# RG-LRU gates with both halves of a block in 128 rows, and a pair of tiles in stages

## The chip, the cores and the metric

The kernel runs on one core of a Trainium2 chip. The metric is the device time of one execution in microseconds (us), median over a few runs.

## The reference

One layer of a decoder trunk for 512 tokens of width 2048, all in fp32: an input projection, a group of RG-LRU recurrences (1024 features) beside a group of eight differential-attention heads, an output projection, a layer norm, a gated MLP with a short convolution, and a second layer norm. What the change touches is the recurrence:

```python
u = _causal_dwconv(rg_x, conv_w, conv_b)
ub = u.reshape(B, S, RG_BLOCKS, RG_BLOCK_DIM)          # 16 blocks of 64 features
r = jax.nn.sigmoid(jnp.einsum('bsgi,gij->bsgj', ub, wa).reshape(B, S, RG_WIDTH) + ba)
ig = jax.nn.sigmoid(jnp.einsum('bsgi,gij->bsgj', ub, wx).reshape(B, S, RG_WIDTH) + bx)
log_a = RG_C * r.astype(jnp.float32) * jax.nn.log_sigmoid(lam.astype(jnp.float32))
a = jnp.exp(log_a)
mult = jnp.sqrt(-jnp.expm1(2.0 * log_a))
bterm = mult * (ig * u).astype(jnp.float32)
_, h = lax.associative_scan(_lru_combine, (a, bterm), axis=1)
```

Each gate of a block is a product of the block's 64 features with a matrix of 64 x 64.

## The kernel before

Features lie in the 128 partitions and tokens in the 512 columns, so a tile of 128 features holds two blocks of 64. Every matmul operand is split into a high and a low half (`split`, lines 101 to 110: ScalarE copies the high half into the reduced format, VectorE subtracts it for the low half), and `mm3` (line 112) makes a product of three matmuls: high by high, low by high, high by low.

The weights come as raw tiles of 128 x 1024 over SyncE's queue, three buffers of them, and are split as they are wanted (`Weights`, lines 155 to 198). The split halves of a weight, `whi` and `wlo`, have three buffers each (W_BUFS): the fourth weight's split waits until TensorE is through with the first's. A weight of 128 x 1024 feeds eight products, 24 matmuls of 512 columns for a projection, 12 for each half of 512.

`PLAN` (line 69) is the order of the projections: values, queries and keys of a head (`qk`), recurrence inputs (`x`), output gates (`g`), and `rec`, the recurrence of a pair of tiles, four in all. Tasks that need several engines (a head's attention, a recurrence) are generators that `spawn` puts beside the projections with a delay; `tick` counts on a modelled time for each product and resumes a task when its time has come. So the text of the program is a mixture of products and small pieces of such tasks. From it a list scheduler in the framework makes the queue of each engine at build time, by the program's order and its own estimate of durations. An engine works its queue off in that order.

A recurrence before is one piece: `recurrence` (line 458) yields only at its end. It makes four gate products for the pair (two tiles by two gates, `mm3` at line 466, weights of 128 x 128 with zeros outside two blocks of 64 x 64), four sigmoids, and then for both tiles in step exp and tanh, the products on VectorE, the root, and two scans. The heads that run beside it have, at the end, a root and a reciprocal of the norm of the head's output (rs, lines 439 and 440), and at the head's start `qk_of` (line 500) makes q and k in halves of 64 rows: k_0 and k_1 hold a component's high half twice, one copied by `split`, the other at line 519, after VectorE's low half at line 518 has been taken.

Of the kernel before, what the change touches and what calls it, by code (L numbers as in the profile page):

```python
# [10 lines left out]
F32 = mybir.dt.float32  # L11
F32R = mybir.dt.float32r
AF = mybir.ActivationFunctionType
ALU = mybir.AluOpType
PSUM = bass.MemoryType.PSUM

P = 128
# [4 lines left out]
RGT = RG // P  # L22
H = 8
DH = 64
# [19 lines left out]
C_FB = C_FW + 2 * FT * 3  # L44
C_LQ = C_FB + 2 * FT
NC_ = C_LQ + 4 * DH


A_BUFS = 56
# [22 lines left out]
def f32(ap):  # L72
    return ap.bitcast(F32)
# [3 lines left out]
def trunk_kernel(ctx, tc, xT, w_qkg, w_v, gate_w, w_out0, w_out, w_up0, w_up, w_down, ln2, consts, out):  # L77
# [17 lines left out]
    def t_tile(dt=F32, name="t"):  # L95
        return tmp.tile([P, S], dt, tag="t", bufs=T_BUFS, name=name)
# [7 lines left out]
    def split(src, hi=None, lo=None, mk=a_tile):  # L104

        hi = mk(F32R, "hi") if hi is None else hi
        lo = mk(F32R, "lo") if lo is None else lo
        nc.scalar.activation(hi, src, AF.Copy)  # L108
        nc.vector.tensor_tensor(lo, src, f32(hi), ALU.subtract)  # L109
        return hi, lo  # L110

    def mm3(ps, w, x, first, last, onto=False):

        for n, (a, b) in enumerate(((w[0], x[0]), (w[0], x[1]), (w[1], x[0]))):
            nc.tensor.matmul(  # L115
                ps, a, b, start=first and n == 0, stop=last and n == 2, skip_group_check=onto
            )
# [85 lines left out]
    def col(i, n=1):  # L203
        return cst[:, i : i + n]
# [240 lines left out]
    def rg_in(j):  # L445
        ps = proj()
        uu = t_tile(F32, "uu")
        nc.scalar.activation(
            uu, ps, AF.Identity, scale=col(C_CONVW + 4 * j + 3), bias=col(C_CONVB + j)
        )  # L450
        for t in range(1, 4):
            nc.vector.scalar_tensor_tensor(
                uu[:, t:], ps[:, : S - t], col(C_CONVW + 4 * j + 3 - t), uu[:, t:],
                ALU.mult, ALU.add,
            )
        return uu, split(uu, mk=t_tile)

    def recurrence(j0, us, w):

        hi, lo = w  # L460
        gates = []
        for i, (uu, s) in enumerate(us):
            for g in range(2):
                c = slice((2 * i + g) * P, (2 * i + g + 1) * P)
                pg = bank()
                mm3(pg, (hi[:, c], lo[:, c]), s, True, True)
                gt = t_tile(F32, "gt")
                nc.scalar.activation(gt, pg, AF.Sigmoid, bias=col((C_BA, C_BX)[g] + j0 + i))  # L468
                gates.append(gt)
        ms, as_ = [], []  # L470
        for i in range(2):
            j, r = j0 + i, gates[2 * i]
            a = t_tile(F32, "a")
            nc.scalar.activation(a, r, AF.Exp, scale=c8[:, j : j + 1])  # L474

            nc.scalar.activation(r, r, AF.Tanh, scale=nc8[:, j : j + 1])
            as_.append(a)
        for i in range(2):
            uu, ig, r, a = us[i][0], gates[2 * i + 1], gates[2 * i], as_[i]
            nc.gpsimd.tensor_tensor(ig, ig, uu, ALU.mult)  # L480
            m = t_tile(F32, "m")
            nc.vector.tensor_tensor(m, a, a, ALU.mult)
            nc.vector.scalar_tensor_tensor(m, m, 1.0, r, ALU.add, ALU.mult)
            ms.append(m)
        for m in ms:
            nc.scalar.activation(m, m, AF.Sqrt)  # L486
        for i in range(2):
            nc.vector.tensor_tensor(ms[i], ms[i], gates[2 * i + 1], ALU.mult)
            hh = a_tile(F32, "hh")
            nc.vector.tensor_tensor_scan(hh, as_[i], ms[i], 0.0, ALU.mult, ALU.add)  # L490
            mix[j0 + i] = hh
        yield 0.0

    def rg_gate(j):
        ps = proj()
# [422 lines left out]
    j = 0  # L918
# [131 lines left out]
def _layout(inputs):  # L1050
    import numpy as np

    g = {k: np.asarray(v) for k, v in inputs.items()}
    f = np.float32

    def tiles(w, cols):

        k = w.shape[0] // P
        w = w.reshape(k, P, -1, P)
        return np.ascontiguousarray(w.transpose(2, 1, 0, 3)[cols]).reshape(len(cols), P, k * P)  # L1060

    a = {}
    a["xT"] = np.ascontiguousarray(g["x"][0].T).reshape(KT, P, S)
    w = g["w_in"][0]
    rgx, rgg = list(range(0, 8)), list(range(8, 16))
    qk = [t for h in range(H) for t in (16 + h, 24 + h)]
    a["w_qkg"] = tiles(w, qk + rgx + rgg)
    wv = w[:, 4096:].reshape(KT // 2, 2, P, 2, 512)
    a["w_v"] = np.ascontiguousarray(wv.transpose(3, 0, 2, 1, 4)).reshape(2, KT // 2, P, 1024)
    gw = np.zeros((RGT // 2, P, 2, 2, P), f)  # L1070
    for i, n in enumerate(("rg_gate_a_w", "rg_gate_x_w")):
        b = g[n][0].reshape(RGT // 2, 2, 2, 64, 64)
        gw[:, :64, :, i, :64] = b[:, :, 0].transpose(0, 2, 1, 3)
        gw[:, 64:, :, i, 64:] = b[:, :, 1].transpose(0, 2, 1, 3)
    a["gate_w"] = gw.reshape(RGT // 2, P, 4 * P)
    wo = g["w_out"][0].reshape(KT, P, D)[ORDER].reshape(D, D)
    a["w_out"] = tiles(wo, list(range(2, KT)))
    w = wo.reshape(KT // 4, 4, P, KT, P)[:, :, :, :2]
    a["w_out0"] = np.ascontiguousarray(w.transpose(0, 2, 1, 3, 4)).reshape(KT // 4, P, 1024)
    up = [t for i in range(FT) for t in (i, FT + i)]  # L1080
    a["w_up"] = tiles(g["w_up"][0], up[4:])
    w = g["w_up"][0].reshape(2, KT // 2, P, 2 * FT, P)[:, :, :, up[:4]]
    a["w_up0"] = np.ascontiguousarray(w.transpose(1, 2, 0, 3, 4)).reshape(KT // 2, P, 1024)
    wd = g["w_down"][0].reshape(FT // 2, 2, P, D // S, S)
    parts, at = [], 0
    for n in CHUNKS:
        w = wd[at // 2 : (at + n) // 2].transpose(3, 0, 2, 1, 4)
        parts.append(w.reshape(-1, P, 2 * S))
        at += n
    a["w_down"] = np.ascontiguousarray(np.concatenate(parts))  # L1090
    a["ln2"] = np.stack([g["ln_ffn_g"][0], g["ln_ffn_b"][0]]).astype(f)
    c = np.zeros((P, NC_), f)

    def put(at, v):
        c[:, at : at + v.shape[1]] = v

    put(C_CONVW, g["rg_conv_w"][0].reshape(4, RGT, P).transpose(2, 1, 0).reshape(P, -1))
    for at, n in ((C_CONVB, "rg_conv_b"), (C_BA, "rg_gate_a_b"), (C_BX, "rg_gate_x_b"),
                  (C_LAM, "rg_lambda"), (C_SUB, "subln_g"), (C_G1, "ln_mix_g"),
                  (C_B1, "ln_mix_b")):  # L1100
        put(at, g[n][0].reshape(-1, P).T)
    fw = g["ffn_conv_w"][0].reshape(3, 2 * FT, P)[:, up]
    put(C_FW, fw.transpose(2, 1, 0).reshape(P, -1))
    put(C_FB, g["ffn_conv_b"][0].reshape(2 * FT, P)[up].T)
    for i, n in enumerate(("lam_q1", "lam_k1", "lam_q2", "lam_k2")):
        put(C_LQ + i * DH, np.broadcast_to(g[n][0], (P, DH)))
    a["consts"] = c
    return a
# [23 lines left out]
```

## Time and profile before

| | us |
|---|---|
| median of 3 runs | 2069.66 (2069.61 to 2070.09) |
| the profiled execution | 2069.49 |
| its span | 2067.7 |
| TensorE busy | 2048.1 (99%) |
| VectorE busy | 1368.9 (66%) |
| ScalarE busy | 1039.5 (50%) |
| GpSimd busy | 181.4 (9%) |

The span is the time from the first to the last instruction; the rest of the execution lies around it. A busy share is a mean over all stages. Of TensorE's matmuls, the pitch from one start to the next is what counts, since they are pipelined: each lasts 0.39 us from start to end while the next one starts well before. The projections and attention, where the recurrences stand, take the first 530 us or so; the rest is the output projection and the MLP.

### The profile page before, as it was taken

What the parts mean: (1) busy time and instruction counts of PE and PEld (TensorE: products, weight loads), DVE (VectorE), ACT (ScalarE), POOL (GpSimd) and SP (SyncE); (2) the same over time, 40 slices, a digit from 0 to 9 for tenths busy, and PEclk for the clock granted to TensorE, in tenths of its full rate; (3) what the DMA queues carried; (4) which work ended last, traced back from release to release, by engine and by line L of the source; (5) the groups of instructions that cost most, each with busy time, mean ns of one, the idle gap of its engine ahead of it and who ended that gap; (6) DMA issues with size and microseconds to landing.
All of it is one profiled execution on the core that took longest, in us unless ns stands there. A gap on an engine that the chain in (4) does not pass through costs nothing.

```text
span 2067.7 us, 28020 instructions
## 1 busy us (share of the span) xinstructions
PE 2048.1 (99%) x10649; PEld 1757.5 (85%) x10649; DVE 1368.9 (66%) x2075; ACT 1039.5 (50%) x1651; POOL 181.4 (9%) x227
## 2 busy tenths in 40 slices
PE   9999999999999999999999999999999999999997
PEld 7888888888888899888888888888888888888886
DVE  6566645768334867888888888888888343333346
ACT  5475735668322656566565566566566232222232
POOL 1000000010122232001001000000100000000000
PEclk9999999999999999999999999999999999999999
DMA  6223222222443246576676676676678643242322
GB/s 221 97 72 97 73 93 85 87 82 91 144 128 128 76 125 167 153 189 171 167 192 170 166 188 176 165 187 178 164 184 283 225 139 116 92 142 92 112 82 82
DMA packets 98152, 288.46 MB, mean 140 GB/s; under 512 B 10209, under 2 KB 18401, under 8 KB 98017
## 3 DMA queue, kind: packets, MB, share of 16 engines
q1 hardware_dynamic: 86496, 244.71, 36.2%
q0 software_dynamic: 11520, 41.95, 11.9%
q8 instruction: 84, 1.38, 0.3%
q14 instruction: 52, 0.42, 0.1%
HBM read 266.70 MB, written 19.92 MB: 139 GB/s over the span
## 4 chain that ended last, share of the span: by engine, by line
PE 94%; ACT 3%; DVE 2%; DMA 1%; issue 1%; DVEq 0%; SPq 0%; ACTq 0%
PE ps L115 54%; PE ps L129 37%; PE ps L359 1%; ACT gt L468 0%; PE ps L360 0%; PE ps L765 0%; ACT s L371 0%; PE ps L389 0%; DVE lo L109 0%; DVE y L621 0%; DMA hid<-hidd 0%; ACT a L474 0%; ACT L486 0%; ACT L474 0%; ACT L468 0%
## 5 line engine op out<-in xcount | busy, mean ns | idle before, releaser
L109 DVE TENSOR_TENSOR wlo<-raw,whi 128x512 fp32r<-128x512 f32 (+1 forms) x676 | 605.2, 913 | 408.6 <-ACT whi L108 407.1
L108 ACT ACTIVATE whi<-raw 128x512 fp32r<-128x512 f32 (+1 forms) x676 | 525.3, 801 | 477.4 <-PE ps L115 376.6
L129 PE MATMUL ps<-hl,whi 128*128 128x512 f32 x1280 | 320.5, 392 | 0.0
L115 PE MATMUL ps<-wlo,hi 128*128 128x512 f32 x768 | 299.5, 390 | 0.6 <-DVE wlo L109 0.6
L115 PE MATMUL ps<-whi,hi 128*128 128x512 f32 x768 | 299.1, 390 | 0.3 <-ACT hi L108 0.3
L115 PE MATMUL ps<-hi,whi 128*128 128x512 f32 (+1 forms) x768 | 298.9, 389 | 0.0
L115 PE MATMUL ps<-whi,lo 128*128 128x512 f32 x768 | 298.7, 389 | 0.0
L115 PE MATMUL ps<-hi,wlo 128*128 128x512 f32 (+1 forms) x768 | 296.6, 386 | 1.2 <-DVE wlo L109 1.2
L115 PE MATMUL ps<-lo,whi 128*128 128x512 f32 (+1 forms) x768 | 296.2, 386 | 0.0
L129 PEld LDWEIGHTS ps<-hl,whi 128*128 128x128 f32 x1280 | 230.2, 189 | 41.1
L129 PE MATMUL ps<-x,whi 128*128 128x512 f32 x960 | 237.2, 389 | 0.0
L129 PEld LDWEIGHTS ps<-x,whi 128*128 128x128 f32 x960 | 180.1, 188 | 37.3
L129 PE MATMUL ps<-hl,wlo 128*128 128x256 f32 x1280 | 173.0, 283 | 0.0
L115 PEld LDWEIGHTS ps<-hi,wlo 128*128 128x128 f32 x768 | 144.3, 188 | 31.3 <-DVE wlo L109 2.4
L115 PEld LDWEIGHTS ps<-whi,hi 128*128 128x128 f32 x768 | 144.3, 188 | 30.9 <-ACT hi L108 1.0
L115 PEld LDWEIGHTS ps<-wlo,hi 128*128 128x128 f32 x768 | 144.4, 188 | 30.8 <-DVE wlo L109 1.0
L115 PEld LDWEIGHTS ps<-whi,lo 128*128 128x128 f32 x768 | 144.4, 188 | 30.0
L115 PEld LDWEIGHTS ps<-lo,whi 128*128 128x128 f32 x768 | 144.5, 188 | 27.5 <-issue 0.2
L129 PEld LDWEIGHTS ps<-hl,wlo 128*128 128x128 f32 x1280 | 164.6, 192 | 3.5 <-ACT cu L878 0.4
L115 PEld LDWEIGHTS ps<-hi,whi 128*128 128x128 f32 x768 | 144.4, 188 | 27.2 <-ACT whi L108 0.2
L129 PEld LDWEIGHTS ps<-x,wlo 128*128 128x128 f32 x960 | 131.0, 190 | 9.4
L807 POOL DMA_DIRECT2D raw<-in_w_up x80 | 69.6, 874 | 735.9 <-DVE raw L827 402.3
(206 smaller groups left out, 2363.8 us busy)
## 6 DMA issues: line engine op xcount, KB each, us to landing
raw<-in_w_up SPq DMA_DIRECT2D x176, 512.0 KB, 5.1
raw<-in_w_down SPq DMA_DIRECT2D x88, 512.0 KB, 3.6
raw<-in_w_up POOLq DMA_DIRECT2D x80, 512.0 KB, 6.8
raw<-in_w_qkg SPq DMA_DIRECT2D x64, 512.0 KB, 3.6
raw<-in_w_out SPq DMA_DIRECT2D x32, 512.0 KB, 3.7
hidd<-cv SPq DMA_DIRECT2D x44, 256.0 KB, 3.9
hid<-hidd SPq DMA_DIRECT2D x44, 256.0 KB, 5.3
raw<-in_w_v SPq DMA_DIRECT2D x15, 512.0 KB, 4.5
```

Source lines behind the costliest of these rows:

```text
L108: nc.scalar.activation(hi, src, AF.Copy)
L109: nc.vector.tensor_tensor(lo, src, f32(hi), ALU.subtract)
L115: nc.tensor.matmul(ps, a, b, start=first and n == 0, stop=last and n == 2, skip_group_check=onto)
L129: nc.tensor.matmul(o, a, b, start=not onto and k == 0, stop=k == len(steps) - 1, skip_group_check=onto)
L359: nc.tensor.matmul(ps[:, :L], qs, k[c][:, :L], start=True, stop=False)
L807: nc.gpsimd.dma_start(self.raw[name], w_up[2 * (self.i - 2) + g][:, n * 1024 : (n + 1) * 1024], accum_op=ALU.add,)
```

## The change

The two halves of a block stand in one operand. For each of a tile's two blocks a `stack` of 128 rows holds the block's high half in the block's own 64 rows and its low half in the other 64. The gate weights are laid out anew: 128 columns for a block, 64 of gate a and 64 of gate x, the same 64 rows of weights in both halves of the partitions. One matmul with the high half of the weights then adds high by high and low by high, and a second one with the low half of the weights, whose rows beside the block's own are set to zero by GpSimd, adds high by low. So two matmuls give both gates of a block, and their result has gate a in the 64 rows of the block and gate x in the other 64 (the columns are exchanged for the second block); the sigmoids take 64 rows each and put them in place.

And the generator now works on one tile after the other and yields three times for each: after the gates, after the products ahead of the root, and after the scan, with 3, 3 and 2 us of modelled time. The work of other tasks and the projections comes between these pieces.

```diff
-        return uu, split(uu, mk=t_tile)
+        stacks = [t_tile(F32R, "st") for _ in range(2)]
+        for st, own, other in zip(stacks, SIDES, SIDES[::-1]):
+            nc.scalar.activation(st[own], uu[own], AF.Copy)
+            nc.vector.tensor_tensor(st[other], uu[own], f32(st[own]), ALU.subtract)
+        return uu, stacks
...
-        gates = []
-        for i, (uu, s) in enumerate(us):
-            for g in range(2):
-                c = slice((2 * i + g) * P, (2 * i + g + 1) * P)
+        for own, block in zip(SIDES[::-1], range(2)):
+            z = f32(lo).rearrange("p (i b c) -> p i b c", i=2, b=2)
+            nc.gpsimd.memset(z[own, :, block, :], 0.0)
+        for i, (uu, stacks) in enumerate(us):
+            j = j0 + i
+            r, ig = gts = [t_tile(F32, "gt") for _ in range(2)]
+            for b, st in enumerate(stacks):
+                c = slice((2 * i + b) * P, (2 * i + b + 1) * P)
                 pg = bank()
-                mm3(pg, (hi[:, c], lo[:, c]), s, True, True)
-                gt = t_tile(F32, "gt")
-                nc.scalar.activation(gt, pg, AF.Sigmoid, bias=col((C_BA, C_BX)[g] + j0 + i))
-                gates.append(gt)
-        ms, as_ = [], []
-        for i in range(2):
-            j, r = j0 + i, gates[2 * i]
+                nc.tensor.matmul(pg, hi[:, c], st, start=True, stop=False)
+                nc.tensor.matmul(pg, lo[:, c], st, start=False, stop=True)
+                own = SIDES[b]
+                for gt, rows, at in zip(gts, (own, SIDES[1 - b]), (C_BA, C_BX)):
+                    nc.scalar.activation(gt[own], pg[rows], AF.Sigmoid, bias=col(at + j)[own])
+            yield 3.0
             a = t_tile(F32, "a")
             nc.scalar.activation(a, r, AF.Exp, scale=c8[:, j : j + 1])
 
             nc.scalar.activation(r, r, AF.Tanh, scale=nc8[:, j : j + 1])
-            as_.append(a)
...
             nc.vector.scalar_tensor_tensor(m, m, 1.0, r, ALU.add, ALU.mult)
-            ms.append(m)
-        for m in ms:
+            yield 3.0
             nc.scalar.activation(m, m, AF.Sqrt)
-        for i in range(2):
-            nc.vector.tensor_tensor(ms[i], ms[i], gates[2 * i + 1], ALU.mult)
+            nc.vector.tensor_tensor(m, m, ig, ALU.mult)
             hh = a_tile(F32, "hh")
-            nc.vector.tensor_tensor_scan(hh, as_[i], ms[i], 0.0, ALU.mult, ALU.add)
-            mix[j0 + i] = hh
-        yield 0.0
+            nc.vector.tensor_tensor_scan(hh, a, m, 0.0, ALU.mult, ALU.add)
+            mix[j] = hh
+            yield 2.0
```

The queues change in the stretch of each of the four recurrences and are the same elsewhere, SyncE's throughout. Three places of the first recurrence follow. In the names, wlo and whi are halves of a projection's weights (the number is the buffer's), rs is the root and then the reciprocal of a head's norm, hh a recurrence's result, s scores, k_n the keys; the changed program's lines are one to eight higher, and its buffers have other numbers.

VectorE's queue about a head's reciprocal (rs), before:

```order
L109 TENSOR_TENSOR lo_1121<-sq_1118,hi_1120 128x512
L509 SCALAR_TENSOR_TENSOR q_1089<-ps_970,q_1089 64x512
L109 TENSOR_TENSOR wlo_1154<-raw_977,whi_1153 128x512 x2
L440 RECIPROCAL rs_1148<-rs_1148 128x512
L109 TENSOR_TENSOR wlo_1199<-raw_1062,whi_1198 128x512
L442 SCALAR_TENSOR_TENSOR mix_1151<-ps_932,subg_86,rs_1148 128x512
L109 TENSOR_TENSOR wlo_1199<-raw_1062,whi_1198 128x512
```

and now:

```order
L110 TENSOR_TENSOR lo_1100<-sq_1097,hi_1099 128x512
L496 SCALAR_TENSOR_TENSOR hh_1105<-a_1045,m_1049 128x512
L110 TENSOR_TENSOR wlo_1149<-raw_981,whi_1148 128x512
L441 RECIPROCAL rs_1143<-rs_1143 128x512
L110 TENSOR_TENSOR wlo_1149<-raw_981,whi_1148 128x512
L443 SCALAR_TENSOR_TENSOR mix_1146<-ps_936,subg_86,rs_1143 128x512
L490 TENSOR_TENSOR m_1166<-a_1162 128x512
L110 TENSOR_TENSOR wlo_1205<-raw_1034,whi_1204 128x512
```

Before, both halves of a low half of weights (wlo_1154) stand ahead of the reciprocal; now one of wlo_1149 stands behind it, and a first product of the second tile (m_1166) comes between it and the next weights.

ScalarE's queue about the copies of k, before:

```order
L439 ACTIVATE rs_1148<-ps_1145,eps_rms_83 128x512
L108 ACTIVATE whi_1230<-raw_1101 128x512 x2
L108 ACTIVATE k_1185<-ps_1094 64x512
L519 ACTIVATE k_1185<-ps_1094 64x512
L108 ACTIVATE k_1186<-ps_1094 64x512
L108 ACTIVATE whi_1289<-raw_1159 128x512 x2
L519 ACTIVATE k_1186<-ps_1094 64x512
```

and now:

```order
L493 ACTIVATE m_1166<-m_1166 128x512
L109 ACTIVATE whi_1295<-raw_1154 128x512 x2
L109 ACTIVATE k_1191<-ps_1073 64x512
L109 ACTIVATE whi_1356<-raw_1210 128x512
L525 ACTIVATE k_1191<-ps_1073 64x512
L109 ACTIVATE k_1192<-ps_1073 64x512
L109 ACTIVATE whi_1356<-raw_1210 128x512
L525 ACTIVATE k_1192<-ps_1073 64x512
```

The first two rows of k_1185, its high half and the copy into the other component's rows, followed each other; now a half of the weights whi_1356 stands between them, and one more between the rows of k_1192.

VectorE's queue about the low halves of k and the scores, before:

```order
L109 TENSOR_TENSOR k_1187<-ps_1094,k_1185 64x512
L109 TENSOR_TENSOR wlo_1231<-raw_1101,whi_1230 128x512 x2
L109 TENSOR_TENSOR k_1188<-ps_1094,k_1186 64x512
L109 TENSOR_TENSOR wlo_1290<-raw_1159,whi_1289 128x512
L362 ISA s_1247,mx_1243<-ps_1244,bias_1241 128x256
L362 ISA mx_1243 128x1
L109 TENSOR_TENSOR wlo_1290<-raw_1159,whi_1289 128x512
L362 ISA s_1252,mx_1243<-ps_1249,bias_1241 128x256
```

and now:

```order
L110 TENSOR_TENSOR wlo_1296<-raw_1154,whi_1295 128x512
L110 TENSOR_TENSOR k_1193<-ps_1073,k_1191 64x512
L110 TENSOR_TENSOR wlo_1357<-raw_1210,whi_1356 128x512
L363 ISA s_1253,mx_1249<-ps_1250,bias_1247 128x256
L363 ISA mx_1249 128x1
L110 TENSOR_TENSOR k_1194<-ps_1073,k_1192 64x512
L110 TENSOR_TENSOR wlo_1357<-raw_1210,whi_1356 128x512
```

Both low halves of k (k_1187, k_1188) stood ahead of the first pass over the scores (s_1247); now the second one (k_1194) stands behind it (s_1253).

## Rows read from the trace of the kernel before

**Rows 1.** The page, busy time, share of span and instructions by engine

```profile
PE 2048.1 (99%) x10649; PEld 1757.5 (85%) x10649; DVE 1368.9 (66%) x2075; ACT 1039.5 (50%) x1651; POOL 181.4 (9%) x227
```

**Rows 2.** Timeline of PE: start us, length us, engine, line, operation, tiles, count

```profile
101.43 0.39 PE L115 MATMUL ps<-hi 128*128 128x512 f32 x1
...
104.15 0.39 PE L115 MATMUL ps<-hi,whi 128*128 128x512 f32 x1
...
108.69 0.60 PE L389 MATMUL ps<-ident,s 128*128 128x128 f32 x4
```

**Rows 3.** Timeline of PE, where starts lie further apart

```profile
118.79 0.51 PE L437 MATMUL ps<-hi,ones_r 128*128 128x512 f32 x1
119.57 0.50 PE L115 MATMUL ps<-hi,wlo 128*128 128x512 f32 x1 [0.27 <-DVE wlo L109]
119.91 0.40 PE L115 MATMUL ps<-hi,whi 128*128 128x512 f32 x1
...
121.29 0.39 PE L115 MATMUL ps<-hi,whi 128*128 128x512 f32 x1
121.61 0.50 PE L437 MATMUL ps<-lo,ones_r 128*128 128x512 f32 x1
...
131.97 0.39 PE L115 MATMUL ps<-hi,wlo 128*128 128x512 f32 x1
132.35 0.39 PE L359 MATMUL ps<-k,q 128*128 128x256 f32 x1
132.57 0.28 PE L360 MATMUL ps<-k,q 128*128 128x256 f32 x1
```

**Rows 4.** Waits of PE, 0 to 540 us: total us, times, longest

```profile
PE ps L115 <- DVE wlo L109: 1.2, 4, 0.3
```

**Rows 5.** Groups, 0 to 540 us: count, busy us, mean ns, idle before

```profile
L468 ACT ACT_TABLE_LOAD x8 | 10.3, 1283 | 0.1
...
L515 POOL MEMSET k<- 64x512 f32 x16 | 8.3, 520 | 1.1 <-PE ps L360 0.2
```

**Rows 6.** Timeline of ACT, first recurrence

```profile
107.15 1.84 ACT L468 ACTIVATE gt<-ps,cst 128x512 f32<-128x512 f32 x3
...
110.30 1.34 ACT L474 ACTIVATE a<-gt,c 128x512 f32<-128x512 f32 x2
...
114.66 1.15 ACT L486 ACTIVATE m<-m 128x512 f32<-128x512 f32 x2
115.72 1.14 ACT L108 ACTIVATE whi<-raw 128x512 fp32r<-128x512 f32 x2
117.15 0.60 ACT L432 ACTIVATE sq<-ps 128x512 f32<-128x512 f32 x1 [0.30 <-PE ps L115]
...
122.21 0.69 ACT L439 ACTIVATE rs<-ps,eps_rms 128x512 f32<-128x512 f32 x1 [0.17 <-PE ps L437]
125.12 1.15 ACT L108 ACTIVATE whi<-raw 128x512 fp32r<-128x512 f32 x2 [2.22 <-PE ps L115]
...
131.72 0.58 ACT L519 ACTIVATE k<-ps 64x512 fp32r<-64x512 f32 x1
```

**Rows 7.** Timeline of DVE, first recurrence

```profile
122.31 1.29 DVE L109 TENSOR_TENSOR wlo<-raw,whi 128x512 fp32r<-128x512 f32 x2
123.53 3.34 DVE L440 RECIPROCAL rs<-rs 128x512 f32<-128x512 f32 x1
...
132.12 0.42 DVE L362 CUSTOM_DVE_ANT_0 s<-ps,bias 128x256 f32<-128x256 f32 x1
132.47 0.08 DVE L362 DVE_READ_ACCUMULATOR2_ANT mx<- 128x1 f32 x1
```

**Rows 8.** Windows: busy us by engine, granted clock, DMA share, GB/s

```profile
700.00:704.00 4.00, 0.86 (x5) 0.62 (x5) 4.00 (x6) 3.74 (x9) 4.00 (x6) 0.93 0.00 0
702.00:712.00 10.00, 7.46 (x43) 7.22 (x43) 10.00 (x21) 7.83 (x20) 3.52 (x5) 0.66 0.21 59
```

More of the change, by code (lines that the diff above doesn't have):

```diff
@@ L46 @@
 NC_ = C_LQ + 4 * DH
+SIDES = [slice(0, DH), slice(DH, P)]
 A_BUFS = 56
@@ L476, in recurrence @@
             nc.scalar.activation(r, r, AF.Tanh, scale=nc8[:, j : j + 1])
-            as_.append(a)
-        for i in range(2):
-            uu, ig, r, a = us[i][0], gates[2 * i + 1], gates[2 * i], as_[i]
             nc.gpsimd.tensor_tensor(ig, ig, uu, ALU.mult)
@@ L483, in recurrence @@
             nc.vector.scalar_tensor_tensor(m, m, 1.0, r, ALU.add, ALU.mult)
-            ms.append(m)
-        for m in ms:
+            yield 3.0
             nc.scalar.activation(m, m, AF.Sqrt)
-        for i in range(2):
-            nc.vector.tensor_tensor(ms[i], ms[i], gates[2 * i + 1], ALU.mult)
+            nc.vector.tensor_tensor(m, m, ig, ALU.mult)
             hh = a_tile(F32, "hh")
-            nc.vector.tensor_tensor_scan(hh, as_[i], ms[i], 0.0, ALU.mult, ALU.add)
-            mix[j0 + i] = hh
-        yield 0.0
+            nc.vector.tensor_tensor_scan(hh, a, m, 0.0, ALU.mult, ALU.add)
+            mix[j] = hh
+            yield 2.0
     def rg_gate(j):
@@ L1069, in _layout @@
     a["w_v"] = np.ascontiguousarray(wv.transpose(3, 0, 2, 1, 4)).reshape(2, KT // 2, P, 1024)
[L1070 to L1075, printed above, removed]
+    gw = np.stack([g[n][0] for n in ("rg_gate_a_w", "rg_gate_x_w")], 2).reshape(RGT // 2, 4, DH, 2, DH)
+    gw[:, 1::2] = gw[:, 1::2, :, ::-1].copy()
+    gw = gw.reshape(RGT // 2, 4, DH, P).transpose(0, 2, 1, 3).reshape(RGT // 2, DH, 4 * P)
+    a["gate_w"] = np.ascontiguousarray(np.concatenate([gw, gw], 1)).astype(f)
     wo = g["w_out"][0].reshape(KT, P, D)[ORDER].reshape(D, D)
```

## The prediction

> **What bounds the kernel now.** The page's first part is read first: TensorE is busy 99% of the span [rows 1], so the time is the number of matmuls times their pitch, plus the places where TensorE stands still. A change to a group of matmuls is therefore worth exactly what it takes from or adds to TensorE's own queue; work on ScalarE and VectorE counts only where TensorE has to wait for it. The timeline of TensorE around the first recurrence comes second. The twelve gate matmuls start at 101.43 and the next product at 104.15 [rows 2], so one costs 2.72 / 12 = 0.227 us, the pitch of every 512-column matmul there. Third, the same engine's timeline where starts are further apart than that pitch [rows 3]: 119.57 comes 0.78 after 118.79 (0.55 lost, on a low half of a weight that VectorE had not yet made), the next start is 0.34 later (0.11 lost, the pipeline filling again), 121.61 comes 0.32 after 121.29 (0.10), 132.35 comes 0.38 after 131.97 (0.15, on a copy of k), and 132.57 comes 0.22 later, where half as many columns should take half the pitch, 0.11 (0.10, rounded down). That is 1.0 us for one recurrence. The view of waits, over the same part of the program, counts the wait for VectorE's wlo four times [rows 4], once for each recurrence, so about 4.0 us are lost now.
>
> **The change, part by part.**
>
> *Gate products.* Twelve matmuls of 512 columns become eight for a pair of tiles; over four pairs 16 go: 16 x 0.227 = 3.6 us off TensorE's queue. The remaining ones have the shape of those in the rows, a weight of 128x128 and 512 columns, so each keeps its 0.227. Of all terms this is the surest.
>
> *Work on half tiles.* The split of a convolved tile was one copy and one subtraction of 128 rows; it is now two of each on 64 rows. The gates were four sigmoids of 128 rows for a pair, and are eight of 64. Work on 64x512 costs what 128x512 costs: the copy of k takes 0.58 [rows 6] against 0.57 for one step of the weight's high half (1.14 for two). So ScalarE gets 2 copies and 4 sigmoids more for each pair, 2 x 0.58 + 4 x 0.61 = 3.6 us (0.61 is a third of the 1.84 row). VectorE gets 2 subtractions more, 1.3 us (half of the 1.29 of two, twice) [rows 7], in time that it has. The two zeroings of 64x2x128 on GpSimd wait for the low half of the gate weights, which is split long before the gate matmuls want it, and are hidden; without that cover they would cost from nothing to twice the 0.52 of the nearest row, a zeroing of 64x512 [rows 5].
>
> *Table loads.* With both tiles in step, sigmoid, exp and sqrt each came in one group. In stages one behind the other they alternate: the changed program has 63 table loads where there were 49, so 14 more, 3 or 4 for each recurrence, at 1.28 us [rows 5]: 18 us more on ScalarE in all. Together with the line above, ScalarE has about 8 us more to do around each recurrence, in a stretch where it was already nearly full.
>
> *What the staging takes away.* In the first wait above, VectorE reached the weight's low half late because two products and two scans of the pair stood ahead of it. They are now one tile's, so this wait and its companions go: 1.0 us for each recurrence, 4.0 in all, taken as gone.
>
> *What it brings.* I follow the three queues in their new order from the first gate matmul, which keeps its place at 101.43. Four gate matmuls and 30 products later the four transposes stand at 101.43 + 34 x 0.227 = 109.14 and end 0.6 later [rows 2]; ScalarE starts the copy of that product at 109.77. Until the root of the attention's norm (rs) ScalarE has, in order, with steps from [rows 5, 6] (a row of two, less the second one's own length, is one step; wt and q are taken as a high half): wt 0.57, load 1.28, exp 0.62, q 0.57, tanh 0.62, high half 0.57, q 0.57, high half 0.57, sq 0.60, load 1.28, sqrt 0.57, hi 0.57, high half 0.57, load 1.28, four sigmoids 2.44, load 1.28. That is 14.0, so rs runs from 123.7 to 124.4 (before: from 122.21). Now three places.
>
> Place A, the reciprocal. Before, both low halves of the next weight (wlo_1154) were made before the reciprocal of 3.34 us [rows 7]; now the second one (wlo_1149) stands behind it, as the first pair of fences on the change shows. The reciprocal starts at 124.4 and the subtraction ends at about 124.4 + 3.34 + 0.6 = 128.35. TensorE, without a stop so far, wants that half at 126.46 (the 118 instructions from 101.43, 102 of 512 columns, 12 of 256 and 4 transposes). It waits 1.9 us. In the third and fourth recurrence the scheduler has exchanged a square and a root, the half behind the reciprocal is that of the following weight, TensorE comes for it at 129.2 and gets it at 130.8: 1.65.
>
> Place B, a copy of k behind a weight's high half. The second pair of fences shows ScalarE's queue: the copy into the other half of k_1191 now stands behind whi_1356. There are three buffers for high halves, so whi_1356 has to wait until TensorE is through with the weight three before it, whose last uses are the instructions just ahead of the score matmuls that want k_1191. How ScalarE stands in such a wait is seen in the row of 125.12 (2.22 us for TensorE) [rows 6]; there no k stood behind it. The loop is: the matmul ends 0.39 after its start [rows 2], some 0.04 for the hand-over (TensorE's start at 132.35 follows the end of a copy of k, 131.72 + 0.58, by that [rows 3, 6]), high half 0.57, copy of k 0.58, 0.04 to TensorE: 1.6 us, where TensorE would have gone on after 0.45. Wait: 1.2.
>
> Place C, the second component of k. On VectorE the low half k_1194 now stands behind the first pass over the scores (s_1253, third pair), which itself needs the score matmuls of place B; ScalarE's last copy of k needs k_1194, and the third score matmul needs that copy. The loop: 0.11 to the second score matmul, 0.28 for it [rows 3], 0.35 and 0.08 for the scores and their maximum [rows 7], 0.65 for k_1194, 0.58 for the copy, and four hand-overs of 0.04: 2.2, where TensorE would have gone on after 0.23. Wait: 2.0. Waits B and C don't shrink when ScalarE is early, since each of them starts at an instruction of TensorE itself.
>
> With 0.11 for the restart after A and after C, a recurrence loses 1.9 + 1.2 + 2.0 + 0.2 = 5.3 us in the first two and 5.1 in the last two: 20.8 us.
>
> *Sum.* 20.8 - 4.0 - 3.6 = +13.2 us on the profiled execution's own 2069.49 (span 2067.7 and 1.8 around it), which is 0.17 below the median: 2082.7 us. Bounds: A falls to nothing if ScalarE is 2 us earlier than I add up, which gives -8.2; it grows by as much as ScalarE is later, and 0.5 us at a transposition some 10 us behind place C may come on top in the first two. B and C could each be off by 0.3 a recurrence from hand-overs, 2.4 in all. If the raw weights land late at place B (their buffers are freed only when VectorE is through with place A's half), up to 1 us more for each, +4.
>
> **The rivals.**
>
> *It does what it says.* The gates cost 3.6 less, the waits of rows 3 go, and the new waits are covered: 2069.5 - 3.6 - 4.0 = 2061.9, faster. For it: TensorE has been kept busy in this stretch by slack I have not followed beyond one recurrence, and a score matmul moved by the scheduler might find k ready. Against it: B and C hang on TensorE's own instructions, and it decides only if both copies of k are ready when TensorE arrives, which the order of the queues excludes. 0.07.
>
> *Only B and C.* A is covered, the rest as summed: 2082.7 - 8.0 = 2074.7. It decides if rs runs 2 us earlier than 123.7. 0.15.
>
> *The clock falls.* The one place in the profile where it fell is at 702 to 712: TensorE had been busy for 0.86 of the 4 us to 704, and the mean granted clock of the ten us from 702 is 0.66 of full speed, that is, a part of them at the lower of 1.2 and 2.4 GHz [rows 8]; (1 - 0.66) x 10 is 3.4 us lost. Behind place B TensorE does two short matmuls between two waits of 1.2 and 2.0. If that sufficed, four falls would add 13.6: 2096. Against it: there TensorE had worked 0.86 in 4 us and stood still again behind them, while here full work stands right ahead of the 3.2 us and right behind. 0.08 for all four, some chance for one.
>
> The Trainium skill, "TensorE: Matmul & The Clock Gate", section "HAM oscillation — how this bites in real kernels", warns that waits between bursts of matmuls let the clock drop again and again, so that every burst starts slow; by that rule the time would be the 2096 just given. The trace agrees that waits can do it once ([rows 8], from 702 on), and no row shows that waits as short as these do.
>
> **How the numbers follow.** The forecast of 2082.7 has 0.65 (2079 to 2087), only B and C 0.15, the clock 0.08, the change as meant 0.07; 0.05 is left for a partial cancelling in which nothing can be measured (0.2%, about 4 us, is what a measurement of this kernel can tell). The range 2073 to 2091 takes in B and C alone and late weights or one or two falls of the clock; it leaves out the faster case and four falls. Faster by over 0.2%: 0.07; within: 0.06; slower: 0.87.
>
> **What would show it.** The profile after should have 16 gate matmuls fewer and 14 table loads more in this part; waits of TensorE for VectorE's low half of about 1.9 us some 25 us behind the first gate matmul of each recurrence; and two waits at the score matmuls, 1.2 for ScalarE's k and 2.0 for the second one, four times each. ScalarE's busy time should grow by some 33 us and VectorE's by 5.5. If TensorE's starts at the score matmuls are at their pitch, B and C are wrong and the forecast with them; if only the wait at the low half is missing, A is. A granted clock below 1.00 between 80 and 450 us would speak for the third rival.

## The result, and the profile after

The changed kernel takes 2093.06 us, median of three runs (2090.72 to 2094.69), against 2069.66: ratio 1.0114, 95% interval 1.0100 to 1.0128. It is slower by 23.4 us, where 13.0 were forecast (2082.7); the forecast's range ended at 2091. The profiled execution took 2093.06 as well (span 2091.0); that is 23.6 above the profiled execution of before, and this is what the traces have to account for.

The page's first part, as in [rows 1]: TensorE has 16 matmuls fewer, ScalarE 36.4 us and VectorE 5.2 us more work (33 and 5.5 were forecast).

```profile
PE 2050.8 (98%) x10633; PEld 1758.2 (84%) x10633; DVE 1374.1 (66%) x2083; ACT 1075.9 (51%) x1689; POOL 184.1 (9%) x235
```

The first matmul of the layer norm behind the output projection, line 577 before and 583 now, started at 531.75 and now starts at 556.11 (first row before, second after): 24.4 us are lost before it, and 0.8 come back behind it.

```profile
531.75 0.70 PE L577 MATMUL ps<-y,ones 128*128 128x512 f32 x1
556.11 0.70 PE L583 MATMUL ps<-y,ones 128*128 128x512 f32 x1
```

The view of TensorE's waits up to there (total us, times, longest), which before had one row that mattered [rows 4]:

```profile
PE ps L360 <- ACT k L525: 13.1, 9, 2.1
PE ps L116 <- DVE wlo L110: 8.4, 4, 2.4
```

The old wait at a weight's low half is gone, and the three forecast places are there. In the first recurrence TensorE's timeline (start, length, in brackets the wait and what ended it) shows all three, and then something that the sum did not have:

```profile
129.22 0.50 PE L116 MATMUL ps<-hi,wlo 128*128 128x512 f32 x1 [2.35 <-DVE wlo L110]
...
138.32 0.39 PE L360 MATMUL ps<-k,q 128*128 128x256 f32 x1 [1.11 <-ACT k L525]
138.54 0.28 PE L361 MATMUL ps<-k,q 128*128 128x256 f32 x1
140.70 0.39 PE L360 MATMUL ps<-k,q 128*128 128x256 f32 x1 [1.88 <-ACT k L525]
...
141.28 0.40 PE L116 MATMUL ps<-lo,whi 128*128 128x512 f32 x1
141.51 0.39 PE L116 MATMUL ps<-hi,wlo 128*128 128x512 f32 x1
...
142.55 0.63 PE L116 MATMUL ps<-hi,whi 128*128 128x512 f32 x1
142.98 0.63 PE L116 MATMUL ps<-lo,whi 128*128 128x512 f32 x1
...
144.68 0.63 PE L116 MATMUL ps<-hi,wlo 128*128 128x512 f32 x1
145.11 0.44 PE L116 MATMUL ps<-hi,whi 128*128 128x512 f32 x1
```

The first three bracketed rows are places A, B and C; each start is 2.51, 1.27 and 2.04 us later than the start ahead of it and the pitch would have it (the brackets count only from the end of what ran before). The rows from 142.55 to 144.68 have nothing in brackets, so nothing is waited for, yet the starts lie 0.43 apart where they lay 0.23 apart a microsecond before, and each matmul lasts 0.63 instead of 0.39. That is TensorE's lower clock, 1.2 instead of 2.4 GHz. The windows (busy us of each engine, then granted clock, DMA share, GB/s) say the same: 0.98 ahead of 142, 0.60 behind it, and the same at the second recurrence.

```profile
136.00:142.00 6.00, 3.02 (x15) 2.14 (x14) 4.18 (x10) 4.36 (x7) 0.00 (x0) 0.98 0.46 150
142.00:146.00 4.00, 4.00 (x14) 3.29 (x14) 1.69 (x7) 2.93 (x6) 0.00 (x0) 0.60 0.37 126
245.00:251.00 6.00, 3.02 (x14) 2.13 (x13) 4.34 (x9) 3.63 (x6) 0.00 (x0) 1.00 0.56 175
251.00:255.00 4.00, 4.00 (x14) 3.30 (x13) 1.54 (x6) 3.67 (x7) 0.00 (x0) 0.57 0.38 131
```

In the first window of each pair TensorE is busy for half of the time, in the second all the time, and there the clock is low: a look at busy time alone would have taken the second window for healthy. The trace's record of the granted clock gives the fall in all four recurrences: 3.41 us at half speed from 141.79, 251.01 and 404.61, and 6.83 us from 462.64.

ScalarE's timeline in the same stretch answers to [rows 6]:

```profile
107.84 2.10 ACT L482 ACTIVATE gt<-ps,cst 64x512 f32<-64x512 f32 x3
...
120.42 2.81 ACT L482 ACTIVATE gt<-ps,cst 64x512 f32<-64x512 f32 x4
...
124.54 0.69 ACT L440 ACTIVATE rs<-ps,eps_rms 128x512 f32<-128x512 f32 x1
...
137.03 0.63 ACT L109 ACTIVATE whi<-raw 128x512 fp32r<-128x512 f32 x1 [2.55 <-PE ps L116]
137.68 0.59 ACT L525 ACTIVATE k<-ps 64x512 fp32r<-64x512 f32 x1
...
140.05 0.59 ACT L525 ACTIVATE k<-ps 64x512 fp32r<-64x512 f32 x1 [0.51 <-DVE k L110]
```

The row of 137.03 is place B as forecast: whi waits 2.55 us for TensorE, the copy of k stands behind it, and TensorE starts 0.05 after that copy's end. VectorE's rows [rows 7] show A (the low half behind the reciprocal) and C (k behind the scores):

```profile
125.27 3.35 DVE L441 RECIPROCAL rs<-rs 128x512 f32<-128x512 f32 x1 [4.09 <-ACT rs L440]
128.53 0.63 DVE L110 TENSOR_TENSOR wlo<-raw,whi 128x512 fp32r<-128x512 f32 x1
...
138.86 0.42 DVE L363 CUSTOM_DVE_ANT_0 s<-ps,bias 128x256 f32<-128x256 f32 x1 [0.48 <-PE ps L361]
139.33 0.69 DVE L110 TENSOR_TENSOR k<-ps,k 64x512 fp32r<-64x512 f32 x1
```

### The profile page after: what moved, and what is told of

The parts are those of the page before. It is cut to its first block, busy times and chain, and to the rows that moved or that the text cites. A ratio compares the mean times of both kernels' runs of the same rounds, so it can differ in the third digit from the quotient of the medians.

```text
span 2091.0 us, 28049 instructions
## 1 busy us (share of the span) xinstructions
PE 2050.8 (98%) x10633; PEld 1758.2 (84%) x10633; DVE 1374.1 (66%) x2083; ACT 1075.9 (51%) x1689; POOL 184.1 (9%) x235
## 4 chain that ended last, share of the span: by engine, by line
PE 92%; ACT 3%; DVE 3%; DMA 1%; issue 1%; SPq 0%; DVEq 0%; ACTq 0%
PE ps L116 53%; PE ps L130 37%; PE ps L360 1%; ACT gt L482 1%; PE ps L361 0%; ACT whi L109 0%; DVE wlo L110 0%; PE ps L390 0%; PE ps L771 0%; DVE rs L441 0%; DVE lo L110 0%; ACT L482 0%; DVE y L627 0%; ACT k L525 0%; DMA hid<-hidd 0%
```

## The experiments

Each kernel was timed beside the kernel before on the same chip, which took 2069.2 to 2070.3 there.

**One part at a time.** The first theory was that the new order of the queues, which the staging had brought, makes the waits, and that the clock falls behind them. Two kernels have one part of the change each. `packed`, against the changed kernel (the line behind ... tells in words what is left out):

```diff
-            yield 3.0
 ...                        # gates of both tiles, then exp and tanh of both, and so on
-            yield 2.0
+        yield 0.0
```

> Only the first part of the change: gates packed (two matmuls for both gates of a block), the recurrence of a pair in one piece, both tiles in step, as before. Theory 1 (the loss comes from three waits that the new order of the queues makes, and from the clock falling behind them): both low halves of the next weight stand ahead of the reciprocal again, and the copies of k follow each other, so none of the three new waits is there, and the clock stays up; 16 matmuls fewer at 0.227 give -3.6: 2066, and up to 4 less if the old waits at the low half shrink too. Rival (the packed gates cost the time: ScalarE works on 64 rows, 24 operations more, at 0.64 to 0.70 each): a good part of the +23 is here too, 2075 to 2090.

Measured: 2088.9, ratio 1.0092 (1.0075 to 1.0108). The theory fell here: the packed gates alone, in the old order of stages, lose 19.6 of the 23.4 us. TensorE's timeline has five waits for each recurrence, all of them on ScalarE or right behind it:

```profile
118.29 0.38 PE L116 MATMUL ps<-wt,hi 128*128 128x256 f32 x1 [0.83 <-ACT wt L396]
119.14 0.39 PE L116 MATMUL ps<-wt,hi 128*128 128x256 f32 x1 [0.46 <-DVE wt L397]
...
121.28 0.50 PE L116 MATMUL ps<-hi,whi 128*128 128x512 f32 x1 [0.56 <-ACT whi L109]
...
123.28 0.50 PE L438 MATMUL ps<-hi,ones_r 128*128 128x512 f32 x1 [1.27 <-ACT hi L109]
124.47 0.50 PE L116 MATMUL ps<-hi,wlo 128*128 128x512 f32 x1 [0.69 <-DVE wlo L110]
```

Against the pitch these five starts are late by 0.99 + 0.72 + 0.72 + 1.44 + 0.96 = 4.83 us. ScalarE's rows show why:

```profile
108.95 4.93 ACT L482 ACTIVATE gt<-ps,cst 64x512 f32<-64x512 f32 x7
...
115.19 1.34 ACT L487 ACTIVATE a<-gt,c 128x512 f32<-128x512 f32 x2
...
117.66 0.58 ACT L396 ACTIVATE wt<-ps 128x512 fp32r<-128x512 f32 x1
```

Seven half sigmoids take 4.93 where three whole ones took 1.84 [rows 6]. The exponential starts at 115.19, before at 110.30 [rows 6]; 1.3 of these 4.9 is this run's later start of the whole program (the copy of wt ahead of the gates stands at 98.83, before at 97.51), the other 3.6 is the half tiles: 3.1 for the sigmoids, the rest for a copy of the second tile. TensorE for its part arrives 4 x 0.227 = 0.9 earlier, since it has four gate matmuls fewer: 3.6 + 0.9 = 4.5, nearly the 4.83. The clock fell in three of the four recurrences (3.41 us each).

`staged` has the gates of before (mm3 with four weights) in the new stages; shown against the changed kernel:

```diff
-            for b, st in enumerate(stacks):
+            for g, gt in enumerate(gts):
...
-                nc.tensor.matmul(pg, hi[:, c], st, start=True, stop=False)
-                nc.tensor.matmul(pg, lo[:, c], st, start=False, stop=True)
+                mm3(pg, (hi[:, c], lo[:, c]), s, True, True)
+                nc.scalar.activation(gt, pg, AF.Sigmoid, bias=col((C_BA, C_BX)[g] + j))
```

> Only the second part: the gates of before (three matmuls for each gate, zero-padded weights), the recurrence tile after tile in stages with 3, 3 and 2. Theory 1: the order decides; in this order the second component of k stands behind the first pass over the scores as in the changed kernel, but the other two places are looser, so TensorE waits some 2.0 four times there, the old waits (4.0) go, and whether the clock falls hangs on the rest: 2070 to 2080. Rival (packed gates alone cost the time): 2066 to 2070, no slower than before. Second rival (14 table loads more are the cost as such): the same loss as in the changed kernel less the gates, 2090 to 2097.

Measured: 2069.85, ratio 1.0005 (0.9996 to 1.0015): no change. The old waits are gone, the first score matmul of the second component (place C) is 1.19 us late in each recurrence, and the clock stays up; its 14 table loads cost nothing that can be measured.

```profile
PE ps L359 <- ACT k L511: 4.3, 5, 1.0
```

So the loss comes with the packed gates, and a second theory took the place of the first: ScalarE's half tiles use up what slack there is, and the order of the queues decides where TensorE meets the lack of it.

**The half tiles without the packing.** `halves` is the kernel before with half-tile work of the same amount on ScalarE and VectorE, and nothing else:

```diff
-        return uu, split(uu, mk=t_tile)
+        for rows in (slice(0, DH), slice(DH, P)):
+            nc.scalar.activation(hi[rows], uu[rows], AF.Copy)
+            nc.vector.tensor_tensor(lo[rows], uu[rows], f32(hi[rows]), ALU.subtract)
...
-                nc.scalar.activation(gt, pg, AF.Sigmoid, bias=col((C_BA, C_BX)[g] + j0 + i))
+                for rows in (slice(0, DH), slice(DH, P)):
+                    nc.scalar.activation(
+                        gt[rows], pg[rows], AF.Sigmoid, bias=col((C_BA, C_BX)[g] + j0 + i)[rows]
+                    )
```

> The kernel before with nothing changed but ScalarE's and VectorE's work on the convolved tiles and the gates: each high half, low half and sigmoid of 128 rows is made as two of 64 rows. The gate matmuls are those of before, three for each gate, and the order of the pair's stages too. Theory 2 (formed on the packed kernel's run: the packed gates lose because ScalarE's 6 operations more for a pair, 0.63 to 0.70 each, 4 us, come out behind one another as TensorE's waits for the copy of the transposed weights, the next high half and the norm's square): the same loss as in the packed kernel without its 3.6 of saved matmuls, that is +19 to +24, 2088 to 2093. Rival (the packed matmuls, their weights or GpSimd's zeroing are what costs): no more than 3 above before, 2069 to 2072.

Measured: 2089.91, ratio 1.0097 (1.0083 to 1.0111). The same loss without one changed matmul, at the same places, and with three falls of the clock. ScalarE's seven half sigmoids take as long as in `packed`, and then TensorE waits:

```profile
107.51 4.91 ACT L473 ACTIVATE gt<-ps,cst 64x512 f32<-64x512 f32 x7
```

```profile
PE ps L437 <- ACT hi L108: 5.1, 4, 1.3
PE ps L115 <- ACT whi L108: 2.7, 4, 0.7
PE ps L115 <- DVE wlo L109: 2.5, 4, 0.7
```

The longest rows are those of `packed`. The packed matmuls, their weights and GpSimd's zeroing are not what costs. No run separates ScalarE's halves from VectorE's; that it is ScalarE is read from the rows, where its sigmoids, one right behind the other, take 3.1 us more than before.

**The order alone.** `delays` is the changed kernel with three other numbers:

```diff
-            yield 3.0
+            yield 8.0
...
-            yield 3.0
+            yield 4.0
...
-            yield 2.0
+            yield 4.0
```

> The changed kernel with three other numbers: the generator's delays are 8, 4 and 4 instead of 3, 3 and 2. Every instruction is the same (61 table loads instead of 63); the lists of the engines are ordered differently: both copies of a k follow each other again, and both low halves of the weight stand ahead of the reciprocal. Theory 1 (the order made the waits, and the clock fell behind them): the three waits of 2.5, 1.3 and 2.0 go but for 0.5 to 1.1 at a score matmul, no fall of the clock; following the queues with the durations of the traces gives some 22 less before the out-projection and 6 to 8 of clock: 2063 to 2068, below the kernel before. Rival (14 table loads and the half tiles are a cost as such, wherever they stand): 2085 to 2095.

Measured: 2065.96 over 11 runs, ratio 0.9981 (0.9972 to 0.9990), faster than the kernel before. It does the same work on the same half tiles, with 61 table loads for 63. TensorE's waits before the out-projection:

```profile
PE ps L360 <- ACT k L525: 1.6, 4, 0.9
```

VectorE now makes the low halves ahead of the reciprocal, and ScalarE has the half sigmoids of the second tile where it waited for TensorE before:

```profile
117.76 0.68 DVE L110 TENSOR_TENSOR wlo<-raw,whi 128x512 fp32r<-128x512 f32 x1
...
120.28 3.35 DVE L441 RECIPROCAL rs<-rs 128x512 f32<-128x512 f32 x1 [1.24 <-ACT rs L440]
```

```profile
126.09 0.58 ACT L109 ACTIVATE k<-ps 64x512 fp32r<-64x512 f32 x1
126.69 2.11 ACT L482 ACTIVATE gt<-ps,cst 64x512 f32<-64x512 f32 x3
128.70 0.58 ACT L525 ACTIVATE k<-ps 64x512 fp32r<-64x512 f32 x1
```

Half sigmoids stand between the two copies of k as well, against what was expected of the order, but they wait for nothing. TensorE is 0.15 late at this k (129.33) instead of 1.27, and 0.32 at the second component's (131.61) instead of 2.04.

**The reciprocal.** `norecip`, the changed kernel without it:

```diff
-        nc.vector.reciprocal(rs, rs)
```

> The changed kernel without the reciprocal of the norm of a head's output (the factor stays the root itself, so the heads' results are another function). It takes away 3.34 of VectorE's work ahead of the second low half of a weight, all else the same in the program. Theory 1: the wait of 2.5 for that half goes in all four recurrences (9.0), the waits at k stay: 2084, or 2076 if the clock, too, falls only behind all three. Rival (the loss is in ScalarE's longer work, table loads and half tiles, whoever waits): that half comes as late, since its high half comes late from ScalarE, and the time is within 3 of 2093.

Measured: 2085.48, ratio 1.0077 (1.0062 to 1.0092). Place A is gone in all four recurrences; B is 1.8, 1.8, 1.8 and 1.4 late, C 2.0 to 2.5, and the clock fell four times. B and C don't need A, and the falls don't either. Together B and C cost 1.4 more than with A there, so that 7.6 of A's 9.0 are gained; in the first recurrence two high halves stand in ScalarE's row between the wait and the copy of k (133.82, 1.15 for both), where the changed kernel had one.

**The clock.** `fill` puts matmuls into the wait of place C:

```diff
                 ps = bank()
                 qs = q[c][:, qb * P : (qb + 1) * P]
+                if c == 1 and qb == 0 and h in (1, 3, 5, 6):
+                    for _ in range(8):
+                        nc.tensor.matmul(ps, q[0][:, :P], k[0], start=True, stop=True)
```

> The changed kernel with 8 matmuls of 512 columns more in TensorE's queue between the first and the second component's score matmuls of the heads beside the recurrences; their result is overwritten by the next matmul, and the output is unchanged. They stand in the wait of 2.0 for the copy of k (8 x 0.227 = 1.8), so TensorE works in it instead of standing; ScalarE's and VectorE's queues are those of the changed kernel. Theory 1a (the clock falls because TensorE stands still in the two waits behind one another, and gives 1.6 back for each fall of 3.4): the falls at 142, 251, 405 and 463 go or shrink, and the time is up to 8 shorter, 2085 to 2088, though nothing is waited for less. Rival 1b (the clock falls for another reason, or the waits grow by what is put in): no change or longer, 2093 to 2100.

Measured: 2087.66, ratio 1.0087 (1.0072 to 1.0102), 5.4 less than the changed kernel though TensorE has 32 matmuls more. The four falls at C are gone. Two others are new, behind place A at 130.16 and 239.39. So 17.06 us at half speed became 6.82; a matmul's step is 0.427 there instead of 0.227, so that 0.47 of such time is lost: 0.47 x 10.24 = 4.8, nearly all of the 5.4 that the traces differ by at the norm's first matmul (550.76 and 556.11). `fill_norecip` takes away A and fills C, and B alone remains:

```diff
-        nc.vector.reciprocal(rs, rs)
...
+                    for _ in range(8):
+                        nc.tensor.matmul(ps, q[0][:, :P], k[0], start=True, stop=True)
```

> The changed kernel without the reciprocal of the head's norm (its results are another function of the heads) and with the 8 matmuls in the place of the third wait: of the three places only the wait for the first copy of k stays, 1.4 to 1.8 in the run without the reciprocal. Theory 1a (the clock falls only where a wait of 2 or more, or two behind one another, leave TensorE standing; the 8 matmuls end that): no fall of the clock in the recurrences; compared with the run without the reciprocal the third wait costs the same (its time is spent in matmuls), and three falls of some 1.6 go: 2080 to 2082. Rival 1b (a single wait of 1.8 is enough): falls stay, 2084 to 2087.

Measured: 2077.31, ratio 1.0032 (1.0021 to 1.0044), 8.2 below `norecip` by the medians, and below the 2080 to 2082 expected. The profiled executions are only 5.4 apart, since this one lost 1.8 at the program's start (the first sigmoid stands at 104.09, in `norecip` at 102.31); from there to the norm it is 7.0 shorter, of which the four falls, 0.47 x 3.41 each, make 6.4. The clock around the first recurrence of `norecip` and then of `fill_norecip`:

```profile
134.00:138.00 4.00, 0.51 (x3) 0.30 (x2) 3.85 (x8) 2.68 (x5) 0.00 (x0) 0.94 0.70 199
138.00:142.00 4.00, 3.88 (x14) 3.40 (x15) 1.29 (x4) 3.94 (x7) 0.00 (x0) 0.63 0.54 187
```

```profile
134.00:138.00 4.00, 2.36 (x12) 1.70 (x11) 4.00 (x7) 3.36 (x7) 0.00 (x0) 1.00 0.49 163
138.00:142.00 4.00, 4.00 (x21) 3.14 (x20) 2.43 (x8) 2.70 (x4) 0.00 (x0) 1.00 0.76 223
```

TensorE waits 1.8 us at B in both; only where it then goes on working, and doesn't wait for C, does the clock stay at full speed. No run has C alone: that its 2.0 would not be enough by itself is concluded from the single waits of A, 1.8 to 2.5 long, behind which the clock mostly stayed up (table below).

**The same kernel again.** `after_again` is the changed kernel, unaltered.

> The changed kernel once more, unaltered, with a second profile. Theory 1: the waits of 2.5, 1.3 and 2.0 stand at the same instructions with the same length within 0.1, since they come from the order of the queues; the falls of the clock, which come from what TensorE did before, may be longer, shorter or missing at one place, and carry the spread of the time (2090.7 to 2094.7 in the three runs, mean clock 0.995 to 0.992). Rival: the waits themselves vary (transfers that land late), and the spread comes from them.

Measured: 2095.39, ratio 1.0121 (1.0106 to 1.0136). The waits stand at the same instructions; in the third recurrence B is 1.27 late instead of the 2.24 of the first profile, all others agree within 0.1. The first recurrence:

```profile
131.14 0.50 PE L116 MATMUL ps<-hi,wlo 128*128 128x512 f32 x1 [2.35 <-DVE wlo L110]
140.25 0.39 PE L360 MATMUL ps<-k,q 128*128 128x256 f32 x1 [1.11 <-ACT k L525]
142.63 0.39 PE L360 MATMUL ps<-k,q 128*128 128x256 f32 x1 [1.88 <-ACT k L525]
```

The one wait that differs bears out the rival at one place: at B of the third recurrence ScalarE's high half waited for a transfer of raw weights in the first profile (first row), and for TensorE in the second:

```profile
400.71 0.63 ACT L109 ACTIVATE whi<-raw 128x512 fp32r<-128x512 f32 x1 [3.83 <-DMA raw<-in_w_qkg]
403.29 0.63 ACT L109 ACTIVATE whi<-raw 128x512 fp32r<-128x512 f32 x1 [4.48 <-PE ps L116]
```

There are five falls now, one of them behind place A of the third recurrence (396.58). So eleven of the twelve waits belong to the program, and the falls vary a little from run to run. But the falls are not all of the spread. This profiled execution is 3.8 longer than the first, and 1.9 of it was there at the first sigmoid (104.94 against 103.02): at the program's start its matmuls of 512 columns step by 0.43 up to 10.6 us, where those of the first profile step by 0.23 from 5.5 on.

```profile
9.35 0.63 PE L116 MATMUL ps<-whi,lo 128*128 128x512 f32 x1
9.78 0.63 PE L116 MATMUL ps<-whi,hi 128*128 128x512 f32 x1
```

**Versions that beat both.** `old_gates_delays` is `staged` with other delays, `rows_moved` has the packed matmuls with whole sigmoids. The first diff is against `staged`, the second against the changed kernel; it leaves out the biases, laid out to fit:

```diff
-            yield 3.0
+            yield 10.0
...
-            yield 3.0
+            yield 5.0
...
-            yield 2.0
+            yield 0.0
```

> The gates of before, staged, with delays of 10, 5 and 0: the second part of the change alone, with other numbers than the 3, 3 and 2 of which the run showed waits of 1.2 at the second score matmul. Theory 1: neither the old waits (4.0) nor the new ones, 2063 to 2066; what the packed gates would save (3.6) is not in it. Rival (the staging gives nothing whatever the numbers, as in the run with 3, 3 and 2): 2069 to 2071.

```diff
-                for gt, rows, at in zip(gts, (own, SIDES[1 - b]), (C_BA, C_BX)):
-                    nc.scalar.activation(gt[own], pg[rows], AF.Sigmoid, bias=col(at + j)[own])
+                nc.scalar.activation(gts[b], pg, AF.Sigmoid, bias=col((C_BA, C_BX)[b] + j))
+            r, ig = gts[0], t_tile(F32, "gt")
+            for own, gt in zip(SIDES, (gts[0], gts[1])):
+                nc.gpsimd.tensor_copy(ig[own], gt[SIDES[gt is gts[0]]])
+            nc.vector.tensor_copy(r[SIDES[1]], gts[1][SIDES[1]])
+            gts = [r, ig]
...
-            yield 3.0
+            yield 6.0
...
-            yield 2.0
+            yield 8.0
```

> The packed gates with two sigmoids of 128 rows for a tile instead of four of 64; the rows that then stand in the wrong half are copied by GpSimd (gate x, two copies of 64 rows) and VectorE (gate a, one), and the biases are laid out to fit. The delays are 6, 3 and 8. Takes 4 x 0.69 = 2.7 us for a pair off ScalarE. Theory 2 (ScalarE's half tiles are what fills the stretch): waits of some 3 in all instead of 5 in the kernel with 8, 4 and 4, 2061 to 2066. Rival (GpSimd's copies come late, 1 us and more each, and the exponential waits for them): 2068 to 2080.

Measured: `old_gates_delays` 2064.11, ratio 0.9975 (0.9964 to 0.9985); `rows_moved` 2064.01, ratio 0.9974 (0.9965 to 0.9983). Neither shows a fall in the recurrences. The first has no wait of TensorE left there at all, which is worth the 4.0 of the old waits and a little more. The second has 3.6 us of matmuls less and still doesn't beat the first measurably; its waits before the out-projection are one of 0.8 and one of 0.2, so most of the 3.6 should show. Its profiled execution, the longest of its eleven (2062.47 to 2066.34), lost some 2.3 at the program's start: from 5 to 12 us TensorE does 18 matmuls there and 27 in `old_gates_delays`, again at a step of 0.43 up to 10.7 us. That is not this kernel's own, since the changed kernel had 25 in one profile and 17 in the other. How many of the unprofiled runs lost it is not known, and why the median shows nothing of the 3.6 stays open.

## Why the prediction was wrong, point by point

The direction and the three places were right. The step that failed is the clock's term, put at nothing: that the clock falls was made a rival with 0.08 for all four, on the argument that full work stands right ahead of the 3.2 us of waits B and C and right behind. It fell in all four recurrences, in both profiles, 17.06 us at half speed in the first, and that makes 8.0 of the 11.4 us by which the sum before the norm was short; A, B and C, sized too small, make the other 3.4 (1.9, 1.3 and 0.2).

| term (us) | forecast | measured |
|---|---|---|
| gate matmuls | -3.6 | -3.6 (16 fewer, same pitch) |
| old waits | -4.0 | -4.0 (gone) |
| place A, four times | 7.1 | 2.51 + 2.52 + 2.20 + 1.81 = 9.0 |
| place B | 4.8 | 1.27 + 1.27 + 2.24 + 1.27 = 6.1 |
| place C | 8.0 | 8.2 |
| restarts | 0.8 | 0.8 (taken as forecast) |
| falls of the clock | 0 | 0.47 x 17.06 = 8.0 |
| sum before the norm | 13.1 (13.2 there, by rounding) | 24.5 (24.4 in the trace) |

*Gates and old waits.* As forecast. The 3.6 are real but small beside what they bring along.

*Half tiles.* The 3.6 us of ScalarE for a pair were right as a sum and wrong as a weight: they entered the forecast only in place A. `packed` and `halves` show that alone they cost some 20 us, since before the change ScalarE had little slack in this stretch (a wait of 0.30 in the rows from 107.15 to 117.15 [rows 6]). The price of one was too low as well: a half sigmoid takes 0.70 in a row (4.93 / 7), not 0.61.

*Place A.* rs started at 124.54, not at 123.7, 0.8 later; the four half sigmoids ahead of it took 2.81 instead of 2.44, which is 0.4 of it, and the program stood 0.2 later from its start (the copy of wt at 109.97, not at 109.77). The low half was ready at 129.16 instead of 128.35; TensorE came for it at 126.7 (126.46 forecast) and waited 2.5, not 1.9.

*Places B and C.* The loops held: C is 2.04 four times (2.0), B 1.27 three times (1.2). That they don't hang on ScalarE's lateness holds for C here, for B only as a lower bound. The 2.24 of the third recurrence is the late raw weights of the forecast's own bound, "up to 1 us more", which happened at one of four places; it was not there in the second profile. In `norecip` both were longer, B up to 1.84 and C up to 2.46.

*The clock.* The rival's price of 3.4 was read rightly from [rows 8], but off a fall of 6.83 us: by the step of the matmuls that costs 3.2. Three of the four falls here lasted 3.41 and cost 1.6 each, so that all four came to 8.0 and not to 13.6. The forecast did take B and C together; what it got wrong is that the work between them, two short matmuls, and the full work around them would keep the clock up. The runs order themselves by what TensorE did just before:

| TensorE's waits (lateness, us) | kernel | falls |
|---|---|---|
| one of 1.2, or smaller ones | staged, delays | 0 of 8 |
| B alone, 1.3 to 2.0 | fill, fill_norecip | 0 of 8 |
| A, 1.8 to 2.5, work behind it | the changed kernel, after_again, fill | 3 of 12 |
| four or five within some 6 us | packed, halves | 6 of 8 |
| B and C, two short matmuls between | the changed kernel, after_again, norecip | 12 of 12 |

The warning that the forecast took from the Trainium skill, "TensorE: Matmul & The Clock Gate", section "HAM oscillation — how this bites in real kernels", that waits between bursts let the clock drop again and again, agrees with the trace: four falls in four recurrences. What no row of before could show is that waits as short as 1.3 and 2.0 do it when they follow each other; behind B alone the clock stayed up eight times out of eight.

*Behind the recurrences.* The fall at the layer norm [rows 8] became shorter, 6.83 us before and 3.41 in the first profile after (it was 6.83 again in the second), which gives back up to 1.6.

*Two slips that change no chance.* With A gone the forecast takes off 8.2 and 8.0, where its own terms give 7.1 and four restarts of 0.11, 7.5. And 702 to 712 is not the one place where the clock of before fell: it is low again from 2061.91 to the end, behind TensorE's last matmul.

*Cause.* The prediction put the waits on the staging. The runs say that neither part does it by itself in the way forecast: the staging with the old gates costs nothing, the packing with the old stages costs 19.6 at other places, and both together with 8, 4 and 4 are 3.2 faster than before. The lost time is ScalarE's half tiles in an order that does not hide them, and the clock that falls behind the waits. Why a scheduler with its own estimate of durations finds such a tight order with 3, 3 and 2 was not tried.

## What to carry to other kernels

Where an engine that is busy half the time on average has little slack in one stretch, work added there is paid nearly in full by the engine that waits for it, as long as the order stays; read the slack in that stretch from its rows, and let every later use feel the delay, not only the one being looked at. Waits that follow each other closely are to be looked at together for the clock, as here the two of 1.3 and 2.0, and a fall costs about half of its length (0.47 here). When a list scheduler orders the queues, its few free numbers (here three delays) are worth trying before a change is judged: they moved this one from 23 us slower to 3 us faster with the same instructions but for two table loads.

## What the runs showed of the hardware that was not expected

- Half-tile sigmoids of ScalarE did not overlap as whole ones do. Three whole ones in a row took 1.84 (0.61 each), three half ones 2.10 and seven 4.93 (0.70 each), though a single one takes 0.69 in both shapes.
- The same kernel's matmuls stepped by 0.43 up to 10.6 us in one profile and by 0.23 from 5.5 us in another, which put 1.9 between the two at the first sigmoid.
- In `rows_moved` VectorE's copies of 64x512 took 0.83 each, longer than its subtractions of 64x512 in the changed kernel (0.69); GpSimd's took 0.63.
